# All eight gates of the mixer run inside its attention, in a written order of TensorE

## The chip, the cores and the metric

The kernel runs on one core of one Trainium2 chip. Its time is the device time of that core in microseconds (us); the median of three runs of the kernel before is 1740.22 us. The core has five instruction engines, each with an in-order queue: TensorE (PE in the profile; its weight loads are PEld), VectorE (DVE), ScalarE (ACT), GpSimd (POOL) and SyncE (SP).

## What is computed

One sequence of 256 tokens with 1024 features goes through two blocks, each with two layers. The first block has layers of retention, sliding-window attention and latent attention side by side, followed by a mixture of 16 experts. The second block has layers of a feed-forward network, a token mixer and another feed-forward network. The change is in the token mixer, and in two helpers that the first block uses too. Cut to the mixer, the reference is:

```python
def token_mixer(u, w_in, b_gate, attn_sink, pool_w, pool_scale, w_br_attn, w_br_pool, w_out, cos, sin):
    proj = u @ w_in
    q, k, v, p, ga, gb = jnp.split(proj, splits, axis=-1)   # 512, 128, 128, 512, 1024, 1024 columns
    q = partial_rope(q, cos, sin)
    k = partial_rope(k, cos, sin)
    y_attn = windowed_gqa(q, k, v, attn_sink) @ w_br_attn   # 8 heads, 2 key heads
    y_pool = multiscale_pool(p, pool_w, pool_scale) @ w_br_pool   # 4 groups of window means
    gate_a = jax.nn.sigmoid(ga + b_gate[:D_MODEL])
    gate_b = jax.nn.sigmoid(gb + b_gate[D_MODEL:])
    return (gate_a * y_attn + gate_b * y_pool) @ w_out
```

In the first block's retention the heads' outputs are normed and multiplied by `silu(g)` and a gain; and its queries and keys are rotated (`rope`) as the mixer's are.

## The kernel before

Weights. All weights lie in one flat fp32 array, in the order in which TensorE uses them; `recipe` (L50) writes that order down. SyncE loads them as tiles of up to 1 MB (`raw`). Each is cut into pieces of up to 1024 columns, and each piece is split into two reduced-precision halves: ScalarE's cast makes `whi` (L350), VectorE's subtraction makes `wlo` (L351). A product then is three matmuls, high by high, high by low, low by high (`mm3`, L413; the profile puts nearly all matmuls on L411, the line of `mm`, so they are told apart by their tiles). Five pieces are in flight; a cast waits until TensorE has used up an older piece.

The mixer (`mixer`, L1298), in the order of its text: normed and transposed input `xT_mx`; queries and keys (`oq`), rotated by `rope` (L625, first product on GpSimd, L628) into `q2r`; `q2r` is split into high and low halves `mT` for the scores, in two rounds j = 0, 1 of three casts on ScalarE (L1332, L1333, L1335) and two subtractions on VectorE (L1334, L1336); values and pooling input (`ovp`, then `vp`, L1341 and L1342). Then eight heads: scores `sc` (four matmuls), softmax (`softmax_head`, L586: masked scores and row extreme on VectorE, L597, exponential on ScalarE, L601, sum and division on VectorE, L608 to L613), four transposes of the probabilities `pt` (L1367), a copy to SBUF (`ptS`, L1371), and the head's output `po` (two matmuls). Two heads share an output bank, which is split into `aT`. Then the pooling, four groups: three matmuls into `opl`, a copy (`pl`, L1385), one matmul out, split into `pTm` (`split_evac`: L496 on ScalarE and L497 on VectorE). Then the gates and the branches: `gate(m)` (L1391) is 2 x 24 matmuls into `ogt`, a scaling on VectorE (L1396) and two tanh on ScalarE; `branch(m)` (L1404) is 12 matmuls over `aT` and 12 over `pTm` into `obr`, a gated product on VectorE (`mg`), the sum of its halves on GpSimd (`msum`, L1411), and a split into `mT`, which the output projection `wo2` (`oz`) reads. There are eight of both; `GATES_AHEAD = 4` sets four gates before the first branch.

The text is not the order on the engines. A scheduler of the framework orders the instructions of each engine by its own estimate of when their inputs are ready, with the order of the text as priority, so that the gates' matmuls, which depend on the input alone, fill the time in which TensorE would wait for softmaxes. Accumulator banks: 4 of the kind `acc` (`sc`, `pt`, `ovp`, `oz`), 2 `mm` (`ogt`, `obr`), 2 `tr` (`po`, `opl`).

The retention (in `attention1`, L633) makes the gate product from `th` (L812, VectorE) and the gain on GpSimd (`gg`, L813), then runs the scores `scr` and the decayed scores `sT` (L824, VectorE) into `oret`.

Of the kernel before, what the change touches and what calls it, by code (L numbers as in the profile page):

```python
# [30 lines left out]
NEG = -1e30  # L31
RAW = 2048
PIECE = 1024
GATES_AHEAD = 4
TAIL = 3
WARM = (24, 12, 60, 20)
LAG = 2
AFFINE_AT = (5, 7, 9, 11)
SCORES_AHEAD = 1
SWA_PERM = [0, 3, 1, 4, 2, 5]  # L40
GQA_PERM = [0, 4, 1, 5, 2, 6, 3, 7]
ROT_ORDER = [*range(8), *range(16, 40), *range(8, 16), *range(40, 64)]
OUT_ORDER = [5, 6, 7, 0, 1, 2, 3, 4]

# [5 lines left out]
def recipe():  # L50
    segs = []

    def wide(name, l, kts, n):
        for kt in kts:
            segs.append((name, l, kt * P, 0, n))

    def blocks(name, l, nkt, bs):
        for b in bs:
            for kt in range(nkt):
                segs.append((name, l, kt * P, b * P, P))  # L60

    for l in range(NL):
        if l == 0:
            for kt in range(0, 8, 2):
                wide("cq", l, range(kt, kt + 2), 384)
                segs.append(None)
        else:
            wide("cq", l, range(8), 384)
        wide("ckv", l, range(8), 288)
        blocks("rqk", l, 8, range(4))  # L70
        wide("vv", l, range(8), 384)
        blocks("uq", l, 3, range(5))
        blocks("ukn", l, 2, range(3))
        wide("ukv", l, range(2), 384)
        blocks("sqk", l, 8, range(4))
        wide("rg", l, range(8), 256)
        wide("wo", l, OUT_ORDER, D)
        segs.append(None)
        for e in range(NE):
            wide("gu", l * NE + e, range(8), 512)  # L80
            wide("dn", l * NE + e, range(2), D)
            segs.append(None)

    def ffn(i, l):
        for f in range(NF):
            blocks(f"f{i}w1", l, 8, [f])
            blocks(f"f{i}w3", l, 8, [f])
            wide(f"f{i}w2", l, [f], D)

    for l in range(NL):  # L90
        ffn(1, l)
        segs.append(None)
        blocks("qk2", l, 8, range(5))
        for kt in range(8):
            for n in range(2):
                segs.append(("vp2", l, kt * P, n * 320, 320))
        for m in range(8 + GATES_AHEAD):
            if m >= GATES_AHEAD:
                blocks("bra", l, 4, [m - GATES_AHEAD])
                blocks("brp", l, 4, [m - GATES_AHEAD])  # L100
            if m < 8:
                blocks("ga", l, 8, [m])
                blocks("gb", l, 8, [m])
        wide("wo2", l, range(8), D)
        segs.append(None)
        ffn(2, l)
        segs.append(None)
    return segs
# [258 lines left out]
def build(ctx: ExitStack, tc: tile.TileContext, ap, tap=None, parts=("b1", "b2")):  # L367
# [12 lines left out]
    def bank(tag, name):  # L380
        return ps.tile([P, 512], F32, name=name, tag=tag, bufs={"acc": 4, "mm": 2, "tr": 2}[tag])
# [14 lines left out]
    def col(name, l, j=None):  # L396
        o, w = COLS[name, l]
        return cols[:, o : o + w] if j is None else cols[:, o + j : o + j + 1]

    def rep(name, l):  # L400
        o, w = REPS[name, l]
        return reps[:, o : o + w]
# [7 lines left out]
    def mm(out, lhsT, rhs, start, stop):  # L410
        return TE.matmul(out, lhsT=lhsT, rhs=rhs, start=start, stop=stop)  # L411
# [213 lines left out]
    def rope(src, swapped, dst, cosT, sinT):  # L625

        shape = [P, src.shape[1], T]
        G.tensor_tensor(out=dst, in0=src, in1=cosT.unsqueeze(1).to_broadcast(shape), op=ALU.mult)  # L628
        V.tensor_tensor(out=swapped, in0=swapped, in1=sinT.unsqueeze(1).to_broadcast(shape), op=ALU.mult)
        return V.tensor_tensor(out=dst, in0=dst, in1=swapped, op=ALU.add)  # L630


    def attention1(l, x, hl, work, cb):  # L633
# [174 lines left out]
        for t in range(2):  # L808

            th = work.tile([P, 256], F32, name="th", tag="rp1", bufs=2)  # L810
            S.activation(out=th, in_=og[t][:, :256], func=AF.Tanh, scale=0.5)
            V.scalar_tensor_tensor(out=th, in0=th, scalar=1.0, in1=og[t][:, :256], op0=ALU.add, op1=ALU.mult)  # L812
            G.tensor_tensor(out=gg[:, t, :], in0=th, in1=rep("gn", l), op=ALU.mult)  # L813
        with tc.issue_after(W.split.ins), tc.issue_after(roped.ins):
            rope(rqk, swapped, rqk, cos64, sin64)
        oret = [bank("acc", f"oret{t}") for t in range(2)]
# [481 lines left out]
    def mixer(h, l, work, cb):  # L1298
# [46 lines left out]
        def scores(i):  # L1345
            b, j = divmod(i, 2)
            sc = bank("acc", "sc2")
            for t in range(2):
                o, c = sc[:, t * T : (t + 1) * T], slice(t * P, (t + 1) * P)
                mm(o, qs[j][:, b, c], ks[:, j], True, False)  # L1350
                mm(o, qs[j][half[j], b, c], kl[half[j]], False, True)
            return sc

        sc = [scores(i) for i in range(SCORES_AHEAD)]
        for b in range(4):
            out = bank("tr", "po2")
            for j in range(2):
                i = 2 * b + j
                if i + SCORES_AHEAD < 8:
                    sc.append(scores(i + SCORES_AHEAD))  # L1360
                pr = softmax_head(
                    work, sc[i], (T, T), (m0, m1), (nsc[:, 0:1], nsc[:, 1:2]), nsink[:, i : i + 1], rep("sink2", l)[:, i : i + 1], "g"
                )
                pt = bank("acc", "pt2")
                for jt in range(2):
                    for it in range(2):
                        TE.transpose(  # L1367
                            pt[:, jt * T + it * P : jt * T + (it + 1) * P], pr[:, it * T + jt * P : it * T + (jt + 1) * P], ident
                        )
                ptS = work.tile([P, 512], F32, name="ptS2", tag="w2k", bufs=2)  # L1370
                S.copy(ptS, pt)  # L1371
                o = out[j * 64 : (j + 1) * 64, :T]
                mm(o, vp[:, 0, half[j]], ptS[:, :T], True, False)
                mm(o, vp[:, 1, half[j]], ptS[:, T:], False, True)
            split_evac(aT[:, 0, b, :], aT[:, 1, b, :], out[:, :T])

        pT = work.tile([P, 2, 4, T], F32R, name="pTm", tag="pTm")
        for g in range(4):
            o = bank("tr", "opl")
            c = slice(P + g * P, P + (g + 1) * P)  # L1380
            mm(o[:, 0:136], vp[:, 0, c], pool[:, 0, g, :], True, False)
            mm(o[:, 120:136], vp[:, 1, c], pool[:, 1, g, :16], False, True)
            mm(o[:, 136:T], vp[:, 1, c], pool[:, 1, g, 16:], True, True)
            pl = work.tile([P, T], F32, name="pl", tag="w1k", bufs=2)
            S.copy(pl, o[:, :T])  # L1385
            mm(o[:, T:], pw[:, g, :], pl, True, True)
            split_evac(pT[:, 0, g, :], pT[:, 1, g, :], o[:, T:], col("pscale", l, g))

        gts = {}

        def gate(m):  # L1391
            o = bank("mm", "ogt")
            gemm_block("ga", hl, 8, o[:, :T])
            gemm_block("gb", hl, 8, o[:, T:])
            gt = work.tile([P, 512], F32, name="gt", tag="gt", bufs=GATES_AHEAD)
            V.tensor_tensor(  # L1396
                out=gt.rearrange("p (b t) -> p b t", b=2), in0=row.unsqueeze(1).to_broadcast([P, 2, T]),
                in1=o.rearrange("p (b t) -> p b t", b=2), op=ALU.mult,
            )
            S.activation(out=gt[:, :T], in_=gt[:, :T], func=AF.Tanh, scale=0.5, bias=hb[:, m : m + 1])  # L1400
            S.activation(out=gt[:, T:], in_=gt[:, T:], func=AF.Tanh, scale=0.5, bias=hb[:, 8 + m : 9 + m])
            gts[m] = gt

        def branch(m):  # L1404
            o = bank("mm", "obr")
            gemm_block("bra", (aT[:, 0], aT[:, 1]), 4, o[:, :T])
            gemm_block("brp", (pT[:, 0], pT[:, 1]), 4, o[:, T:])
            mg = work.tile([P, 512], F32, name="mg", tag="w2k", bufs=2)
            V.scalar_tensor_tensor(out=mg, in0=gts.pop(m), scalar=1.0, in1=o, op0=ALU.add, op1=ALU.mult)
            ms = work.tile([P, T], F32, name="msum", tag="w1k", bufs=2)  # L1410
            G.tensor_tensor(out=ms, in0=mg[:, :T], in1=mg[:, T:], op=ALU.add)  # L1411
            split_evac(ml[0][:, m, :], ml[1][:, m, :], ms, 0.5)

        for m in range(8 + GATES_AHEAD):
            if m >= GATES_AHEAD:
                branch(m - GATES_AHEAD)
            if m < 8:
                gate(m)
        oo = [[bank("acc", f"oz{t}{n}") for n in range(2)] for t in range(2)]
        gemm_wide(  # L1420
            "wo2", ml, 8, [[(oo[t][n], n * 512, (n + 1) * 512) for n in range(2)] for t in range(2)], tail=TAIL
# [110 lines left out]
```

## Time and profile before

| | |
|---|---|
| three runs | 1740.22 us median, 1735.24 to 1745.57 |
| profiled run | 1737.47 us, its span 1735.7 us |
| mean granted TensorE clock | 0.983 |
| TensorE busy | 1662.0 us, 96% |
| VectorE busy | 1251.6 us, 72% |
| ScalarE busy | 985.8 us, 57% |
| GpSimd busy | 62.4 us, 4% |
| DMA | 331.85 MB, mean 191 GB/s |

A time in the trace counts from the span's start. Of the 1735.7 us the two mixers' stretches from the first gate to the output projection begin at 873.6 (layer 0) and 1414.0 (layer 1). A row of the timeline gives the start, the length, the engine, the line, the instruction and the tiles out<-in; where several in a row are alike they are one row with a count, and the bracket behind it is the idle time before it and what ended that. The ends of matmuls are modelled, so a pace is better read from start to start. [...]

### The profile page before, as it was taken

What the parts mean: (1) busy time and instruction counts of PE and PEld (TensorE: products, weight loads), DVE (VectorE), ACT (ScalarE), POOL (GpSimd) and SP (SyncE); (2) the same over time, 40 slices, a digit from 0 to 9 for tenths busy, and PEclk for the clock granted to TensorE, in tenths of its full rate; (3) what the DMA queues carried; (4) which work ended last, traced back from release to release, by engine and by line L of the source; (5) the groups of instructions that cost most, each with busy time, mean ns of one, the idle gap of its engine ahead of it and who ended that gap; (6) DMA issues with size and microseconds to landing.
All of it is one profiled execution on the core that took longest, in us unless ns stands there. A gap on an engine that the chain in (4) does not pass through costs nothing.

```text
span 1735.7 us, 24721 instructions
## 1 busy us (share of the span) xinstructions
PE 1662.0 (96%) x9258; PEld 1407.9 (81%) x9258; DVE 1251.6 (72%) x2268; ACT 985.8 (57%) x1643; POOL 62.4 (4%) x54
## 2 busy tenths in 40 slices
PE   8998999899999979999999999998999999999997
PEld 7877777797777758888889888887888798978886
DVE  5768999876789997666675666667666766666665
ACT  5646777564577755555475555555555565555553
POOL 0001000200100010000000100000000000100000
PEclk9998999999899989999999999999999999999999
DMA  9432999543278965555433545554555442545540
GB/s 379 148 120 100 339 335 347 189 169 122 74 296 335 333 224 199 179 189 189 153 129 132 189 164 185 191 194 146 190 182 186 166 161 90 188 176 194 191 149 25
DMA packets 49421, 331.85 MB, mean 191 GB/s; under 512 B 5648, under 2 KB 5904, under 8 KB 13712
## 3 DMA queue, kind: packets, MB, share of 16 engines
q1 hardware_dynamic: 47952, 325.73, 52.2%
q10 hardware_dynamic: 1344, 4.49, 0.9%
q8 instruction: 75, 1.23, 0.3%
q14 instruction: 50, 0.41, 0.1%
HBM read 326.79 MB, written 1.05 MB: 189 GB/s over the span
## 4 chain that ended last, share of the span: by engine, by line
PE 66%; DVE 3%; ACT 2%; issue 1%; ACTq 0%; DVEq 0%
PE v L411 14%; PE u L411 14%; PE f L411 14%; PE ogt L411 6%; PE ogu L411 4%; PE obr L411 3%; PE oz L411 2%; PE yg L411 2%; PE ovp L411 2%; PE oq L411 2%; PE sc L411 1%; PE po L411 1%; DVE wlo L351 1%; ACT junk L537 1%; PE opl L411 1%
## 5 line engine op out<-in xcount | busy, mean ns | idle before, releaser
L351 DVE TENSOR_TENSOR wlo<-raw,whi 128x1024 fp32r<-128x1024 f32 (+2 forms) x611 | 736.6, 1212 | 351.7 <-ACT whi L350 345.8
L350 ACT CAST whi<-raw 128x1024 fp32r<-128x1024 f32 (+2 forms) x611 | 629.7, 1034 | 533.5 <-PE v L411 125.8
L411 PE MATMUL f<-whi,fhh 128*128 128x512 f32 x704 | 233.0, 392 | 4.3 <-ACT fhh L1284 4.3
L411 PE MATMUL u<-xT_f,whi 128*128 128x512 f32 x528 | 191.1, 401 | 4.0 <-DVE xT_f L497 4.0
L411 PE MATMUL v<-xT_f,whi 128*128 128x512 f32 x528 | 189.9, 399 | 0.0
L411 PEld LDWEIGHTS f<-whi,fhh 128*128 128x128 f32 x704 | 132.1, 188 | 36.6 <-ACT fhh L1284 6.0
L411 PE MATMUL u<-xT_f,wlo 128*128 128x256 f32 x528 | 149.0, 282 | 0.0
L411 PE MATMUL v<-xT_f,wlo 128*128 128x256 f32 x528 | 148.3, 281 | 0.0
L411 PE MATMUL f<-wlo,fhh 128*128 128x512 f32 x352 | 138.1, 392 | 0.0
L411 PEld LDWEIGHTS u<-xT_f,whi 128*128 128x128 f32 x528 | 100.1, 190 | 28.2 <-DVE xT_f L497 4.7
L411 PEld LDWEIGHTS v<-xT_f,whi 128*128 128x128 f32 x528 | 99.2, 188 | 24.7
L411 PE MATMUL ogu<-wlo,xgh 128*128 128x512 f32 x256 | 102.2, 399 | 3.9 <-DVE wlo L351 3.9
L411 PE MATMUL ogu<-whi,xgh 128*128 128x512 f32 x256 | 102.8, 402 | 0.1
L411 PEld LDWEIGHTS u<-xT_f,wlo 128*128 128x128 f32 x528 | 100.5, 190 | 2.4
L411 PE MATMUL ogu<-whi,xgl 128*128 128x512 f32 x256 | 101.2, 395 | 0.0
L411 PEld LDWEIGHTS v<-xT_f,wlo 128*128 128x128 f32 x528 | 99.8, 189 | 0.0
L411 PE MATMUL ogt<-xT_mx,whi 128*128 128x256 f32 x512 | 97.4, 287 | 0.0
L411 PE MATMUL yg<-whi,hh 128*128 128x512 f32 x256 | 84.9, 393 | 2.9 <-ACT hh L493 2.8
L411 PEld LDWEIGHTS ogt<-xT_mx,whi 128*128 128x128 f32 x512 | 80.4, 191 | 3.0 <-issue 1.5
L411 PEld LDWEIGHTS f<-wlo,fhh 128*128 128x128 f32 x352 | 66.1, 188 | 10.5
L411 PE MATMUL ogt<-xT_mx,wlo 128*128 128x256 f32 x256 | 73.0, 286 | 0.0
L411 PE MATMUL u<-x2hl,whi 128*128 128x512 f32 x176 | 64.7, 406 | 6.2 <-DVE x2hl L584 6.2
(555 smaller groups left out, 3078.9 us busy)
## 6 DMA issues: line engine op xcount, KB each, us to landing
raw<-in_wflat_dram SPq DMA_DIRECT2D x276, 1024.0 KB, 4.8
raw<-in_wflat_dram SPq DMA_DIRECT2D x10, 960.0 KB, 4.6
gb<-in_rows_dram SPq DMA_DIRECT2D x8, 512.0 KB, 4.7
raw<-in_wflat_dram SPq DMA_DIRECT2D x4, 992.0 KB, 4.8
raw<-in_wflat_dram SPq DMA_DIRECT2D x4, 512.0 KB, 3.4
raw<-in_wflat_dram SPq DMA_DIRECT2D x2, 1008.0 KB, 6.3
raw<-in_wflat_dram SPq DMA_DIRECT2D x2, 976.0 KB, 6.9
raw<-in_wflat_dram SPq DMA_DIRECT2D x4, 384.0 KB, 5.9
```

Of the source, the lines that this page charges most:

```text
L350: nc.scalar.copy(hi[:, :n], r[:, c : c + n])
L351: self.split = nc.vector.tensor_tensor(out=lo[:, :n], in0=r[:, c : c + n], in1=hi[:, :n].bitcast(F32), op=ALU.subtract)
L411: return TE.matmul(out, lhsT=lhsT, rhs=rhs, start=start, stop=stop)
L537: S.activation(out=junk(), in_=h[:, t, n * 512 : (n + 1) * 512], func=AF.Square, accum_out=ss[:, n : n + 1])
```

## The change

The order of TensorE from the first gate to the last branch is now written out by hand, under `tc.manual_schedule(engines={mybir.EngineType.PE})`; the other engines' order is still the scheduler's. The gates are cut in halves `ga` and `gb` and set around the parts of a head: for head i, the scores of head i+1, on every second head the pooling into its bank, `gb` of gate i, pooling out, the transposes of head i, `ga` of gate i+1, the output of head i. After head 7's transposes come two pool branches, the last output, and then the branches in the order of `BRANCHES`. The flat weight array follows in that order, and a branch's bank takes the pool half first. The first product of the rotation, the retention's `gg` and the branch sum `msum` move from GpSimd to VectorE. Gates have eight buffers instead of four. A smaller scratch area for dynamic DMAs, which this kernel has none of from GpSimd, frees memory.

```diff
-GATES_AHEAD = 4
...
-SCORES_AHEAD = 1
...
+BRANCHES = [("brp", 0), ("brp", 1), ("bra", 0), ("bra", 1)] + [(k, m) for m in range(2, 8) for k in ("brp", "bra")]
@@ -94,13 +93,11 @@
         for kt in range(8):
             for n in range(2):
                 segs.append(("vp2", l, kt * P, n * 320, 320))
-        for m in range(8 + GATES_AHEAD):
-            if m >= GATES_AHEAD:
-                blocks("bra", l, 4, [m - GATES_AHEAD])
-                blocks("brp", l, 4, [m - GATES_AHEAD])
-            if m < 8:
-                blocks("ga", l, 8, [m])
-                blocks("gb", l, 8, [m])
+        for m in range(8):
+            blocks("ga", l, 8, [m])
+            blocks("gb", l, 8, [m])
+        for k, m in BRANCHES:
+            blocks(k, l, 4, [m])
         wide("wo2", l, range(8), D)
         segs.append(None)
         ffn(2, l)
@@ -625,7 +622,7 @@
     def rope(src, swapped, dst, cosT, sinT):
 
         shape = [P, src.shape[1], T]
-        G.tensor_tensor(out=dst, in0=src, in1=cosT.unsqueeze(1).to_broadcast(shape), op=ALU.mult)
+        V.tensor_tensor(out=dst, in0=src, in1=cosT.unsqueeze(1).to_broadcast(shape), op=ALU.mult)
         V.tensor_tensor(out=swapped, in0=swapped, in1=sinT.unsqueeze(1).to_broadcast(shape), op=ALU.mult)
         return V.tensor_tensor(out=dst, in0=dst, in1=swapped, op=ALU.add)
 
@@ -810,7 +807,7 @@
             th = work.tile([P, 256], F32, name="th", tag="rp1", bufs=2)
             S.activation(out=th, in_=og[t][:, :256], func=AF.Tanh, scale=0.5)
             V.scalar_tensor_tensor(out=th, in0=th, scalar=1.0, in1=og[t][:, :256], op0=ALU.add, op1=ALU.mult)
-            G.tensor_tensor(out=gg[:, t, :], in0=th, in1=rep("gn", l), op=ALU.mult)
+            V.tensor_tensor(out=gg[:, t, :], in0=th, in1=rep("gn", l), op=ALU.mult)
         with tc.issue_after(W.split.ins), tc.issue_after(roped.ins):
             rope(rqk, swapped, rqk, cos64, sin64)
         oret = [bank("acc", f"oret{t}") for t in range(2)]
@@ -1351,16 +1348,67 @@
                 mm(o, qs[j][half[j], b, c], kl[half[j]], False, True)
             return sc
 
-        sc = [scores(i) for i in range(SCORES_AHEAD)]
-        for b in range(4):
-            out = bank("tr", "po2")
-            for j in range(2):
-                i = 2 * b + j
-                if i + SCORES_AHEAD < 8:
-                    sc.append(scores(i + SCORES_AHEAD))
+        pT = work.tile([P, 2, 4, T], F32R, name="pTm", tag="pTm")
+        gts = {}
+
+        def pool_in(g):
+
+            o = bank("tr", "opl")
+            c = slice(P + g * P, P + (g + 1) * P)
+            mm(o[:, 0:136], vp[:, 0, c], pool[:, 0, g, :], True, False)
+            mm(o[:, 120:136], vp[:, 1, c], pool[:, 1, g, :16], False, True)
+            mm(o[:, 136:T], vp[:, 1, c], pool[:, 1, g, 16:], True, True)
+            pl = work.tile([P, T], F32, name="pl", tag="w1k", bufs=2)
+            S.copy(pl, o[:, :T])
+            return o, pl
+
+        def pool_out(g, o, pl):
+            mm(o[:, T:], pw[:, g, :], pl, True, True)
+            split_evac(pT[:, 0, g, :], pT[:, 1, g, :], o[:, T:], col("pscale", l, g))
+
+        def gate(m, o):
+            gt = work.tile([P, 512], F32, name="gt", tag="gt", bufs=8)
+            V.tensor_tensor(
+                out=gt.rearrange("p (b t) -> p b t", b=2), in0=row.unsqueeze(1).to_broadcast([P, 2, T]),
+                in1=o.rearrange("p (b t) -> p b t", b=2), op=ALU.mult,
+            )
+            S.activation(out=gt[:, :T], in_=gt[:, :T], func=AF.Tanh, scale=0.5, bias=hb[:, m : m + 1])
+            S.activation(out=gt[:, T:], in_=gt[:, T:], func=AF.Tanh, scale=0.5, bias=hb[:, 8 + m : 9 + m])
+            gts[m] = gt
+
+        obr = {}
+
+        def branch(k, m):
+            if k == "brp":
+                obr[m] = bank("mm", "obr")
+                gemm_block("brp", (pT[:, 0], pT[:, 1]), 4, obr[m][:, T:])
+                return
+            o = obr.pop(m)
+            gemm_block("bra", (aT[:, 0], aT[:, 1]), 4, o[:, :T])
+            mg = work.tile([P, 512], F32, name="mg", tag="w2k", bufs=2)
+            V.scalar_tensor_tensor(out=mg, in0=gts.pop(m), scalar=1.0, in1=o, op0=ALU.add, op1=ALU.mult)
+            ms = work.tile([P, T], F32, name="msum", tag="w1k", bufs=2)
+            V.tensor_tensor(out=ms, in0=mg[:, :T], in1=mg[:, T:], op=ALU.add)
+            split_evac(ml[0][:, m, :], ml[1][:, m, :], ms, 0.5)
+
+
+        with tc.manual_schedule(engines={mybir.EngineType.PE}):
+            og = bank("mm", "ogt")
+            gemm_block("ga", hl, 8, og[:, :T])
+            ahead = scores(0)
+            for i in range(8):
+                b, j = divmod(i, 2)
+                sc, ahead = ahead, scores(i + 1) if i < 7 else None
                 pr = softmax_head(
-                    work, sc[i], (T, T), (m0, m1), (nsc[:, 0:1], nsc[:, 1:2]), nsink[:, i : i + 1], rep("sink2", l)[:, i : i + 1], "g"
+                    work, sc, (T, T), (m0, m1), (nsc[:, 0:1], nsc[:, 1:2]), nsink[:, i : i + 1], rep("sink2", l)[:, i : i + 1], "g"
                 )
+                if j == 0:
+                    pooled = pool_in(b)
+                gemm_block("gb", hl, 8, og[:, T:])
+                gate(i, og)
+                if j == 0:
+                    pool_out(b, *pooled)
+                    out = bank("tr", "po2")
                 pt = bank("acc", "pt2")
                 for jt in range(2):
                     for it in range(2):
@@ -1369,53 +1417,19 @@
                         )
                 ptS = work.tile([P, 512], F32, name="ptS2", tag="w2k", bufs=2)
                 S.copy(ptS, pt)
+                if i < 7:
+                    og = bank("mm", "ogt")
+                    gemm_block("ga", hl, 8, og[:, :T])
+                else:
+                    branch(*BRANCHES[0])
+                    branch(*BRANCHES[1])
                 o = out[j * 64 : (j + 1) * 64, :T]
                 mm(o, vp[:, 0, half[j]], ptS[:, :T], True, False)
                 mm(o, vp[:, 1, half[j]], ptS[:, T:], False, True)
-            split_evac(aT[:, 0, b, :], aT[:, 1, b, :], out[:, :T])
-
...
-        for m in range(8 + GATES_AHEAD):
-            if m >= GATES_AHEAD:
-                branch(m - GATES_AHEAD)
-            if m < 8:
-                gate(m)
+                if j == 1:
+                    split_evac(aT[:, 0, b, :], aT[:, 1, b, :], out[:, :T])
+            for k, m in BRANCHES[2:]:
+                branch(k, m)
         oo = [[bank("acc", f"oz{t}{n}") for n in range(2)] for t in range(2)]
         gemm_wide(
             "wo2", ml, 8, [[(oo[t][n], n * 512, (n + 1) * 512) for n in range(2)] for t in range(2)], tail=TAIL
@@ -1519,7 +1533,7 @@
     import concourse.bacc as bacc
     from concourse.bass_utils import run_bass_kernel_spmd
 
-    nc = bacc.Bacc("TRN2", target_bir_lowering=False, num_devices=1)
+    nc = bacc.Bacc("TRN2", target_bir_lowering=False, num_devices=1, dynamic_dma_scratch_size=1024)
     arrays, ap = {}, {}
     for name, v in host_arrays(inputs).items():
         arrays[f"in_{name}_dram"] = v
```

TensorE before, in the mixer of layer 0 from the middle of gate 0 to the first head's output (`sc_9090`, `sc_9096`, `sc_9124` are the scores of heads 0, 1 and 2, `pt` the transposed probabilities, `po` a head's output, `ogt` the gate):

```order
L411 MATMUL sc_9090<-mT 128x256 x4
L411 MATMUL ogt<-xT_mx,whi 128x256
...
L411 MATMUL sc_9096<-mT 128x256 x4
...
L1367 MATMUL pt_9115<-cperm,pr_g 128x128
L411 MATMUL sc_9124<-mT 128x256
L1367 MATMUL pt_9115<-cperm,pr_g 128x128 x3
L411 MATMUL sc_9124<-mT 128x256 x3
...
L411 MATMUL po_9095<-ptS_9120,vp 64x256 x2
L1367 MATMUL pt_9143<-cperm,pr_g 128x128 x4
```

TensorE now, same place, from the end of the first half of gate 0 (`sc_9122`, `sc_9127`, `sc_9228` are the scores of heads 0, 1 and 2, `opl` the pooling, whose constants `cb_6990` holds):

```order
L408 MATMUL ogt<-xT_mx,wlo 128x256
L408 MATMUL sc_9122<-mT 128x256 x4
L408 MATMUL sc_9127<-mT 128x256 x4
L408 MATMUL opl<-cb_6990,vp 128x136
L408 MATMUL opl<-cb_6990,vp 128x16
L408 MATMUL opl<-cb_6990,vp 128x120
L408 MATMUL ogt<-xT_mx,whi 128x256 x2
...
L408 MATMUL opl<-pl,pw 128x256
L1415 MATMUL pt_9190<-cperm,pr_g 128x128 x4
...
L408 MATMUL po_9189<-ptS_9195,vp 64x256 x2
L408 MATMUL sc_9228<-mT 128x256 x4
```

The scores of heads 0 and 1 now stand back to back behind 24 gate matmuls, with the first pooling behind them; the transposes of head 0 stand right behind the pooling's last product, and the scores of head 2 behind the first head's output.

VectorE before, in the same place, from the last of head 1's row extremes on (`gt` is the scaled gate, `den_g`, `rec_g` and `pr_g` the softmax's sum, its reciprocal and the probabilities):

```order
L597 ISA pr_g,nm_g<-sc_9096,cb_6990,nsink_8768,nsc 128x256
L597 ISA nm_g 128x1
L1396 TENSOR_TENSOR gt<-row,ogt 128x512
L351 TENSOR_TENSOR wlo<-raw,whi 128x1024
L608 TENSOR_TENSOR den_g<-den_g,es_g 128x2
L351 TENSOR_TENSOR wlo<-raw,whi 128x1024
L609 RECIPROCAL rec_g<-den_g 128x2
L608 TENSOR_TENSOR den_g<-den_g,es_g 128x2
L351 TENSOR_TENSOR wlo<-raw,whi 128x1024
L613 TENSOR_SCALAR pr_g<-pr_g,rec_g 128x256 x2
```

VectorE now, same place (`pTm` is the low half of the pooled group's split):

```order
L594 ISA pr_g,nm_g<-sc_9127,cb_6990,nsink_8768,nsc 128x256
L594 ISA nm_g 128x1
L348 TENSOR_TENSOR wlo<-raw,whi 128x1024
L605 TENSOR_TENSOR den_g<-den_g,es_g 128x2
L1371 TENSOR_TENSOR gt<-row,ogt 128x512
L606 RECIPROCAL rec_g<-den_g 128x2
L494 SCALAR_TENSOR_TENSOR pTm<-opl,cols,pTm 128x256
L610 TENSOR_SCALAR pr_g<-pr_g,rec_g 128x256 x2
```

The gate's scaling moved from ahead of the softmax's sum to between the sum and its reciprocal, and the pooled group's split came in ahead of the division of head 0's probabilities; two of three weight splits went from this place.

## Rows read from the trace of the kernel before

**Rows 1.** Busy times by window: us, each engine, granted clock, DMA share, GB/s.

```profile
873.60:970.20 96.60, 96.60 (x706) 86.28 (x705) 62.47 (x126) 58.40 (x116) 4.76 (x7) 1.00 0.36 126
1414.00:1510.70 96.70, 96.70 (x707) 86.38 (x706) 62.18 (x124) 57.57 (x115) 4.81 (x7) 1.00 0.36 124
960.00:970.00 10.00, 10.00 (x86) 10.00 (x85) 6.36 (x9) 5.31 (x8) 1.60 (x3) 1.00 0.51 176
```

**Rows 2.** Timeline of TensorE: a gate's first matmuls, then two branches' first (start, us).

```profile
953.09 0.40 PE L411 MATMUL ogt<-xT_mx,whi 128*128 128x256 f32 x2
...
958.84 0.40 PE L411 MATMUL obr<-aT,whi 128*128 128x256 f32 x2
...
961.69 0.40 PE L411 MATMUL obr<-aT,whi 128*128 128x256 f32 x2
```

**Rows 3.** Timeline of TensorE: a head's small products, and a pooling group's.

```profile
889.16 1.08 PE L411 MATMUL po<-ptS,vp 128*64 128x256 f32 x4
...
890.17 0.66 PE L1367 MATMUL pt<-cperm,pr_g 128*128 128x128 f32 x4
890.58 1.30 PE L411 MATMUL sc<-mT 128*128 128x256 f32 x4
...
915.18 0.94 PE L411 MATMUL opl<-cb,vp 128*128 128x136 f32 x6
...
915.88 0.36 PE L411 MATMUL ogt<-xT_mx,wlo 128*128 128x256 f32 x1
...
916.80 0.60 PE L411 MATMUL opl<-pl,pw 128*128 128x256 f32 x2
```

**Rows 4.** Timeline of TensorE: layer 0's first gate matmuls and first scores.

```profile
873.62 0.40 PE L411 MATMUL ogt<-xT_mx,whi 128*128 128x256 f32 x2
...
877.70 1.22 PE L411 MATMUL sc<-mT 128*128 128x256 f32 x4
```

**Rows 5.** Timeline of ScalarE: the weight cast ahead of the query's copies.

```profile
873.38 1.05 ACT L350 CAST whi<-raw 128x1024 fp32r<-128x1024 f32 x1 [2.03 <-PE ovp L411]
```

**Rows 6.** Timeline of VectorE: the query's splits, head 0's softmax, gate 0's scaling.

```profile
876.26 1.22 DVE L1336 TENSOR_TENSOR mT<-q2r,mT 64x1024 fp32r<-64x1024 f32 x1 [0.61 <-ACT mT L1335]
...
878.16 1.22 DVE L1336 TENSOR_TENSOR mT<-q2r,mT 64x1024 fp32r<-64x1024 f32 x1 [0.24 <-ACT mT L1335]
...
879.88 0.54 DVE L597 CUSTOM_DVE_ANT_0 pr_g<-sc,cb,nsink 128x256 f32<-128x256 f32 x1
...
882.09 0.68 DVE L1396 TENSOR_TENSOR gt<-row,ogt 128x512 f32<-128x512 f32 x1
...
886.30 0.61 DVE L613 TENSOR_SCALAR pr_g<-pr_g,rec_g 128x256 f32<-128x256 f32 x2
```

**Rows 7.** The pooling's tile by instruction: count, ns min/median/max, first and last start.

```profile
L496 ACT ACTIVATE pTm<-opl,cols x8: 467/474/475, 917.5 to 1467.1; 128x256 fp32r<-128x256 f32 x8
L497 DVE SCALAR_TENSOR_TENSOR pTm<-opl,cols,pTm x8: 477/484/484, 918.0 to 1468.4; 128x256 fp32r<-128x256 f32 x8
```

**Rows 8.** Timeline: retention of the first block's layer 1, before the head outputs.

```profile
405.56 0.75 DVE L812 SCALAR_TENSOR_TENSOR th<-th,og 128x256 f32<-128x256 f32 x2
...
406.22 0.55 DVE L824 TENSOR_TENSOR sT<-scr,cb 128x384 f32<-128x384 f32 x1
...
406.83 0.88 PE L411 MATMUL oret<-vv,sT 128*128 128x64 f32 x6 [0.48 <-DVE sT L824]
```

**Rows 9.** Timeline of GpSimd and VectorE: the mixer's rotation and weight splits beside it.

```profile
860.38 2.97 POOL L628 TENSOR_TENSOR q2r<-q,cb 128x1280 f32<-128x1280 f32 x1 [214.02 <-DVE q L1320]
...
860.65 4.79 DVE L351 TENSOR_TENSOR wlo<-raw,whi 128x960 fp32r<-128x960 f32 x2 [0.48 <-ACT whi L350]
...
865.36 1.48 DVE L629 TENSOR_TENSOR q2s<-q2s,cb 128x1280 f32<-128x1280 f32 x1
...
866.76 1.21 DVE L351 TENSOR_TENSOR wlo<-raw,whi 128x1024 fp32r<-128x1024 f32 x1
```

**Rows 10.** Busy times by window, at the entry of the mixer in layers 0 and 1.

```profile
844.00:846.00 2.00, 2.00 (x12) 2.00 (x11) 1.44 (x8) 1.39 (x4) 0.00 (x0) 0.50 0.00 0
1384.00:1386.00 2.00, 1.45 (x11) 1.28 (x12) 2.00 (x14) 0.95 (x3) 0.00 (x0) 1.00 0.00 0
```

More of the change, by code (lines that the diff above doesn't have):

```diff
@@ L1374, in mixer @@
                 mm(o, vp[:, 1, half[j]], ptS[:, T:], False, True)
-            split_evac(aT[:, 0, b, :], aT[:, 1, b, :], out[:, :T])
[L1377 to L1412, printed above, removed]
```

## The prediction

> **What bounds the kernel now.** I read first the busy time by engine: TensorE 96% of the span, VectorE 72%, ScalarE 57%, GpSimd 4%. So TensorE sets the time, and an edit counts only if it gives TensorE less work, takes away one of its waits, or adds one. Then I read the two stretches that the change rewrites, the mixer of layer 0 and of layer 1 from the first gate to the output projection: 96.6 us each, TensorE busy in all of it at a granted clock of 1.00, VectorE busy 62 us and the DMA engines 0.36 of the time [rows 1]. The reader is to see that nothing is waited for there: no wait can be taken out of these stretches, only new ones put in.
>
> The third look is at what "busy" hides, since an end of a matmul is modelled. Start to start, a gate of 48 matmuls takes 958.84 - 953.09 = 5.75 us (0.12 us each), a branch 961.69 - 958.84 = 2.85 us [rows 2]. Eight of both are 68.8 us. The small products: a head's output 1.01 us, the transposes 0.41, the scores 1.22, so 2.64 a head and 21.1 for eight; the pooling 0.70 into the bank and at most 0.60 out of it, 5.2 for four groups [rows 3, 4]. Together 95.1; the other 1.5 us of 96.6 are what some 19 interruptions of the gate stream cost, about 0.08 us each.
>
> **TensorE's work after.** The same matmuls, none more or less. In the new order the stream of gate and branch blocks is interrupted 16 times a layer: -3 x 0.08 = -0.2 us, -0.4 for both layers. Bounds: all 1.5 us of both layers gone, -3; or as much again, +3. I take -0.4, by the 0.08 just found.
>
> **The start of the attention, where the order is now fixed.** Before, the scheduler put each head's products where their inputs were ready, with gate matmuls between. Now TensorE has to take: the first half of gate 0, scores 0, scores 1, the first pooling, the second half of gate 0, pooling out, transposes 0. Times of layer 0:
>
> 1. Scores 0. The half gate begins at 873.62 [rows 4] and ends 24 x 0.12 = 2.87 later, at 876.5. The scores need the second part of q's split, which ended at 876.26 + 1.22 = 877.48 and was itself released by ScalarE [rows 6]. ScalarE was late since a weight cast stands ahead of q's copies in its queue and waited 2.03 us for the value projection to free a piece [rows 5]; neither the cast nor its place changes. The scheduler put the scores at 877.70 [rows 4] and filled up with gate matmuls; the written order can't. Wait: 877.55 - 876.5 = 1.05 us.
> 2. Scores 1 follow 1.22 later, at 878.75, but use the other half of q: 878.16 + 1.22 = 879.4 [rows 6]. Wait: 0.7.
> 3. Transposes 0. Scores 1 end at 880.65, the pooling at 881.35, the half gate at 884.2, pooling out at 884.8. The probabilities could be ready by then (row maxima 0.54 us each from scores 0 at 878.8, and before the first head had 6.4 us from its first maximum at 879.88 to its division at 886.30, other work between [rows 6]). But VectorE's new queue has two instructions ahead of the division: gate 0's scaling (0.68 us, from 884.2) and the second half of the pooled group's split, which waits for pooling out at 884.8, then 0.47 us on ScalarE and 0.48 on VectorE [rows 6, 7]: 885.75. The division of both halves takes 0.61: 886.35. Wait: 886.35 - 884.8 = 1.55. Behind the waiting transpose stand gate 1 and all the rest; no other engine is short of work by it.
>
> Sum 3.3 us a layer. Layer 1 runs the same program on the same row lengths, so 6.6 for two. Bounds from the same rows: nothing at all (the splits and the division just in time, as every head's were before [rows 1]), or twice, 13, if each wait also takes the 2.03 of the cast's wait with it. I take 6.6; with the -0.4 it is 6.2.
>
> **The heads that follow** cost nothing, and this is what hides them: between a head's scores and its transposes TensorE now has half a gate, transposes, half a gate, a head's output, scores and half a gate: 2.87 + 0.41 + 2.87 + 1.01 + 1.22 + 2.87 = 11.3 us. The softmax before took 6.4 with weight splits between its steps [rows 6]. Without that cover each head would cost its lateness (rival C).
>
> **The branches at the end.** Without gates between them, eight branches make VectorE's densest stretch. The last four stood alone before as well: in 960 to 970 VectorE was busy 6.36 of 10 us [rows 1]. The branch sum is new on it: 10/2.85 = 3.5 an interval, at the 0.48 of the nearest row of that shape [rows 7] 1.7 us, so 8.1 of 10: still free. The sum leaves GpSimd, which did three in that interval in 1.60 us; nobody on TensorE waited for them. The weight pieces are not short: the cast waits for TensorE to free a piece, not for data [rows 5], and the DMA engines are at 0.51 of their time [rows 1]; the stream's new order moves no byte more. Cost 0. Bounds 0 to +3 us, one branch's time, should the first attention branch come before its last head is split. The four more gate buffers and the smaller scratch hold no work of an engine: 0.
>
> **The two moves of the retention.** The swish product, now on VectorE, stands between the row maths on `th` and the first decay product `sT`. TensorE waits there already: 0.48 us for `sT` at 406.83, behind two `th` instructions that took 406.22 - 405.56 = 0.66 in all [rows 8]. Two products of the same shape at that price add 0.66 to that wait in layer 1. In layer 0 the wait was smaller and I take half: 0.33. Together 1.0 (bounds 0, if gate weights split elsewhere give the room, to 1.5).
>
> **The rotation.** GpSimd took 2.97 us for the mixer's first product; meanwhile two weight splits of 960 columns took 4.79 us on VectorE where one of 1024 takes 1.21 [rows 9]. So the engine that was to be relieved lost 4.79 - 2.3 = 2.5 us. The same product on VectorE is 1.48 by the sister row [rows 9], so VectorE gains about 1 us. [...] It is worth nothing in the sum, since the wait that follows is set by ScalarE's cast [rows 5], not by VectorE; two of these in the mixers and two in the first block. Bounds -2 (1 us each where it counts, on one layer of each block) to +1.
>
> **Sum** against the profiled run: 1737.5 + 6.2 + 1.0 = 1744.7. The median shown, 1740.2, lies 2.7 above that run, so I predict 1747.
>
> **Rivals.**
>
> A. The waits don't come, or are paid back: VectorE, rid of the contention, reaches the splits sooner and TensorE enters the heads as smoothly as before. For it: the 2.5 us above, and that every head was hidden before [rows 1]. Against it: the splits wait on ScalarE, and the order of the queues. Then the sum is -0.4 to +1.0 with up to -2 for the rotation: 1739, between 1734 and 1742. It is also the case in which the change doesn't do what it says: TensorE has no idle time there for gates to fill.
>
> B. The new gaps bring the clock down. At the mixer's entry of layer 0 TensorE has gaps of this size, and the granted clock was 0.50 in 844 to 846 after them; in layer 1 the same gaps kept 1.00 [rows 10]. [...]
>
> C. Slower, by late softmaxes: the written order stops TensorE at every head if VectorE's queue puts a division behind a gate's scaling and weight splits. The place is the transposes of heads 1 to 7, 14 in two layers; the price 0.5 us, nearly one scaling [rows 6], each: +7, 1754. It decides from the point where a softmax takes 11.3 us; before it took 6.4, hence improbable.
>
> **How the numbers follow.** Forecast 55% (1742 to 1752), A 22%, B 15% (1748 to 1756), C 8% (1750 to 1760). The range 1736 to 1757 leaves out the lower part of A and the upper parts of B and C. What a measurement of this kernel tells from no change is about 0.5%, so 1731.5 and 1748.9. Faster than that would need all bounds of gain at once: 7%. Slower: a third of the forecast, most of B and C: 36%. The rest, 57%, within.
>
> **What would show it.** In the profile after: TensorE idle before `sc` released by VectorE's q split, about 1 and 0.7 us; before the first `pt`, released by the division, about 1.5 us, at the start of both attentions and nowhere later; `oret` waiting about 1.1 us in layer 1; no GpSimd row in the mixers; weight splits at 1.2 us beside the rotation. From the first gate to the output projection 99.7 instead of 96.6 us. I am wrong if these stretches are no longer than before, if waits come at later heads or in the branches, or if the clock falls in them.

## The result and the profile after

| | before | after |
|---|---|---|
| median | 1740.30 us (8 runs, 1735.01 to 1745.57) | 1753.36 us (8 runs, 1749.80 to 1757.63) |
| profiled run | 1737.47 us, clock 0.983 | 1757.63 us, clock 0.975 |

The changed kernel is slower: ratio 1.0073, 95% interval 1.0057 to 1.0089, or 12.7 us. The profiled run lost more, 20.2 us, and a part of that is luck: it was the slowest of its eight runs, and the profiled run before was below the median. So the trace says where time was lost, and only repeated runs say how much.

The page of the changed kernel shows as much TensorE time as before in share, more in microseconds, and GpSimd halved (busy us, share, instructions):

```profile
PE 1677.3 (96%) x9258; PEld 1419.2 (81%) x9258; DVE 1261.0 (72%) x2292; ACT 985.4 (56%) x1643; POOL 34.6 (2%) x30
```

The same 9258 matmuls are 15 us longer, and the mean granted clock is 0.975 instead of 0.983: where busy time rises and the count doesn't, look at the clock by stretches. The two mixers from the first gate to `wo2`, then three stretches inside them and in the retention (window, busy times, granted clock as a share of full speed, DMA share, GB/s; compare [rows 1]):

```profile
880.08:981.68 101.60, 98.71 (x706) 87.96 (x705) 66.34 (x133) 58.21 (x116) 0.00 (x0) 0.98 0.36 120
1427.74:1530.75 103.01, 100.11 (x707) 88.98 (x705) 66.00 (x131) 58.34 (x116) 0.00 (x0) 0.97 0.34 116
886.00:892.00 6.00, 6.00 (x31) 5.49 (x32) 4.63 (x12) 4.31 (x12) 0.00 (x0) 0.72 0.41 124
1432.00:1442.00 10.00, 9.32 (x40) 7.67 (x39) 6.34 (x15) 6.06 (x15) 0.00 (x0) 0.66 0.31 107
412.00:422.00 10.00, 9.36 (x35) 7.48 (x32) 2.92 (x9) 0.00 (x0) 0.00 (x0) 0.55 0.32 105
```

The mixers took 101.6 and 103.0 us instead of 96.6. TensorE is idle for 2.9 of it in each (101.60 - 98.71), and it ran part of the rest at a lower clock: 6 us at 0.72 are 1.7 us lost, 10 us at 0.66 are 3.4. 96.6 + 2.9 + 1.7 = 101.2, and 96.6 + 2.9 + 3.4 = 102.9; 0.1 to 0.4 remains, which these windows don't explain. The waits themselves, in layer 0:

```profile
883.99 1.32 PE L408 MATMUL sc<-mT 128*128 128x256 f32 x4 [0.87 <-DVE mT L1333]
885.99 1.29 PE L408 MATMUL sc<-mT 128*128 128x256 f32 x4 [0.68 <-DVE mT L1333]
887.22 1.41 PE L408 MATMUL opl<-cb,vp 128*128 128x136 f32 x6
...
892.41 0.59 PE L408 MATMUL opl<-pl,pw 128*128 128x256 f32 x2
894.35 0.81 PE L1415 MATMUL pt<-cperm,pr_g 128*128 128x128 f32 x4 [1.35 <-DVE pr_g L610]
```

They are where the forecast put them: 0.87, 0.68 and 1.35 us for a predicted 1.05, 0.7 and 1.55. The slow stretch begins at the end of the second wait or just behind it, and is over before the third. Behind the third, the longest, the clock stays at 1.00, in layer 0 as in layer 1 (where the third ends at 1443.4):

```profile
887.00:891.00 4.00, 4.00 (x20) 3.87 (x21) 3.63 (x9) 3.33 (x11) 0.00 (x0) 0.57 0.38 88
892.00:900.00 8.00, 6.65 (x43) 5.07 (x42) 5.92 (x12) 3.92 (x7) 0.00 (x0) 1.00 0.48 169
1433.00:1441.00 8.00, 7.35 (x30) 6.48 (x31) 5.26 (x13) 5.08 (x13) 0.00 (x0) 0.57 0.39 134
1441.00:1450.00 9.00, 7.65 (x50) 5.94 (x49) 6.53 (x15) 3.94 (x8) 0.00 (x0) 1.00 0.43 131
```

VectorE's queue at the third shows its cause, the gate's scaling and the pooled split ahead of the division:

```profile
892.61 0.69 DVE L1371 TENSOR_TENSOR gt<-row,ogt 128x512 f32<-128x512 f32 x1 [1.98 <-PE ogt L408]
...
893.55 0.48 DVE L494 SCALAR_TENSOR_TENSOR pTm<-opl,cols,pTm 128x256 fp32r<-128x256 f32 x1 [0.18 <-ACT pTm L493]
...
893.95 0.61 DVE L610 TENSOR_SCALAR pr_g<-pr_g,rec_g 128x256 f32<-128x256 f32 x2
```

Over the whole span TensorE's waits for these releasers are (us in total, times, longest):

```profile
PE sc L408 <- DVE mT L1333: 3.1, 4, 0.9
PE oret L408 <- DVE sT L821: 2.9, 4, 1.2
PE pt L1415 <- DVE pr_g L610: 2.7, 2, 1.3
```

The first and the third did not exist before; the second was

```profile
PE oret L411 <- DVE sT L824: 1.3, 3, 0.6
```

No later head and no branch waits. In the retention of layer 1 the gain product stands between `th` and `sT` as forecast, and lengthens the wait of [rows 8] from 0.48 to 1.15 us:

```profile
409.35 0.75 DVE L810 TENSOR_TENSOR gg<-th,reps 128x256 f32<-128x256 f32 x2
410.02 0.55 DVE L821 TENSOR_TENSOR sT<-scr,cb 128x384 f32<-128x384 f32 x1
...
410.62 0.88 PE L408 MATMUL oret<-vv,sT 128*128 128x64 f32 x6 [1.15 <-DVE sT L821]
```

Behind it comes the slow stretch 412 to 422, which no step of the forecast had: from `scr` to `trr` the retention of layer 1 took 432.35 - 407.79 = 24.6 us, before 423.88 - 404.66 = 19.2. Layer 0's retention has a slow stretch too, and took 20.8 us from `scr` to `trr` instead of 18.3:

```profile
99.00:102.00 3.00, 3.00 (x12) 2.61 (x11) 0.98 (x2) 0.00 (x0) 0.00 (x0) 0.51 0.04 11
```

The rotation, last, went as its rows let expect; beside it the two weight splits of 960 columns took 1.15 and 1.16 us instead of 4.79 together [rows 9]. Nothing came of that: from the first `oq` to the first gate TensorE took 1414.08 - 1382.27 = 31.8 us in layer 1 before, and 880.08 - 848.26 = 31.8 in layer 0 now, both at a clock of 1.00.

```profile
866.73 1.49 DVE L625 TENSOR_TENSOR q2r<-q,cb 128x1280 f32<-128x1280 f32 x1
...
868.14 1.15 DVE L348 TENSOR_TENSOR wlo<-raw,whi 128x960 fp32r<-128x960 f32 x1
...
870.53 1.16 DVE L348 TENSOR_TENSOR wlo<-raw,whi 128x960 fp32r<-128x960 f32 x1 [1.24 <-ACT whi L347]
```

### The profile page after: what moved, and what is told of

The parts are those of the page before. It is cut to its first block, busy times and chain, and to the rows that moved or that the text cites. A ratio compares the mean times of both kernels' runs of the same rounds, so it can differ in the third digit from the quotient of the medians.

```text
span 1755.8 us, 24673 instructions
## 1 busy us (share of the span) xinstructions
PE 1677.3 (96%) x9258; PEld 1419.2 (81%) x9258; DVE 1261.0 (72%) x2292; ACT 985.4 (56%) x1643; POOL 34.6 (2%) x30
## 3 DMA queue, kind: packets, MB, share of 16 engines
HBM read 326.79 MB, written 1.05 MB: 187 GB/s over the span
## 4 chain that ended last, share of the span: by engine, by line
PE 66%; DVE 3%; ACT 2%; issue 1%; ACTq 0%; DVEq 0%
PE u L408 14%; PE v L408 14%; PE f L408 14%; PE ogt L408 5%; PE ogu L408 4%; PE obr L408 3%; PE oz L408 2%; PE yg L408 2%; PE oq L408 2%; PE ovp L408 2%; PE sc L408 1%; PE po L408 1%; DVE wlo L348 1%; PE opl L408 1%; ACT whi L347 1%
## 5 line engine op out<-in xcount | busy, mean ns | idle before, releaser
L408 PEld LDWEIGHTS v<-xT_f,whi 128*128 128x128 f32 x528 | 99.2, 188 | 24.6
L408 PE MATMUL ogu<-whi,xgl 128*128 128x512 f32 x256 | 101.6, 397 | 0.0
```

## The experiments

Theory 1: the loss is the new waits and slow stretches that they bring on. Theory 2: the waits alone; slow stretches fall by luck, as often without them. Theory 3: a steady cost of the written order or of VectorE's new work.

**The moves alone.** `G.` becomes `V.` for rotation, gain product and branch sum; the order stays the scheduler's.

```diff
-        G.tensor_tensor(out=dst, in0=src, in1=cosT...
+        V.tensor_tensor(out=dst, in0=src, in1=cosT...
-            G.tensor_tensor(out=gg[:, t, :], in0=th...
+            V.tensor_tensor(out=gg[:, t, :], in0=th...
-            G.tensor_tensor(out=ms, in0=mg[:, :T]...
+            V.tensor_tensor(out=ms, in0=mg[:, :T]...
```

> Only the three moves from GpSimd to VectorE, on the kernel before. Theory 1 (the loss is the new waits and the slow clock that they bring on): both retentions wait some 0.6 us more for sT and their clock falls to 0.50 for some microseconds afterwards; mixers stay at 96.6 us; +2 to +7 us in all, ratio 1.001 to 1.004. Theory 2 (the waits alone; the clock falls as often without them): +1.3 us, ratio 1.001, no slow stretch in the retentions that the kernel before doesn't have. Theory 3 (a steady cost of VectorE's added work): the mixers are longer too, each 1 us or more.

1743.28 us, ratio 1.0018 (1.0000 to 1.0037). The mixers are as before, layer 1's retention is slow, and layer 0's stays at 1.00:

```profile
879.51:976.06 96.55, 96.55 (x707) 86.28 (x705) 65.23 (x133) 58.23 (x116) 0.00 (x0) 1.00 0.37 126
1420.08:1516.61 96.53, 96.53 (x706) 86.27 (x705) 64.87 (x131) 57.46 (x116) 0.00 (x0) 1.00 0.36 123
410.00:422.00 12.00, 11.36 (x40) 9.03 (x40) 3.61 (x11) 0.00 (x0) 0.00 (x0) 0.50 0.24 87
```

VectorE does the branch sums and the rotation, and the mixers are not a tenth longer: theory 3 falls for them, and the 5 to 6 us of each mixer belong to the written order.

**The gain product back on GpSimd**, all else as changed.

> The changed kernel with the retention's gain product back on GpSimd. Theory 1: 3 to 8 us less than the changed kernel, ratio to the kernel before 1.003 to 1.006, the retentions at a clock of 1.00 as before. Theory 2: 1.3 us less, ratio 1.0065. Theory 3: no less, 1.007.

1750.77 us, ratio 1.0054 (1.0032 to 1.0076). Over all runs its mean is 4.0 us (2.4 to 5.7) below the changed kernel's; the waits that it takes away are 2.9 - 1.3 = 1.6 us. Its mixers have the waits, and both are slow; its retention isn't, in either layer (layer 1 shown last):

```profile
871.00:972.60 101.60, 98.70 (x707) 87.96 (x706) 66.35 (x133) 58.24 (x116) 0.00 (x0) 0.98 0.35 120
1417.60:1519.19 101.59, 98.69 (x707) 87.85 (x705) 66.00 (x131) 58.24 (x116) 0.00 (x0) 0.98 0.35 117
400.00:424.00 24.00, 22.16 (x133) 17.66 (x132) 16.50 (x52) 9.00 (x18) 2.73 (x3) 1.00 0.30 104
```

**Half a gate more ahead.** Both halves of gate 0 stand ahead of the first scores, and each later half one place earlier; the first pool branch takes the place that comes free at head 7.

```diff
+            half_gate()
+            half_gate()
             ahead = scores(0)
...
-                gemm_block("gb", hl, 8, og[:, T:])
-                gate(i, og)
+                half_gate()
...
-                if i < 7:
-                    og = bank("mm", "ogt")
-                    gemm_block("ga", hl, 8, og[:, :T])
-                else:
-                    branch(*BRANCHES[0])
-                    branch(*BRANCHES[1])
+                half_gate()
```

> The changed kernel with the second half of gate 0 ahead of the first scores, and every later half gate one place earlier. Theory 1: no wait for the first two scores, a wait of at most 0.7 us before the first transposes, no slow clock: mixers 96.6 to 97.5 us instead of 101.6 and 103.0, 8 to 11 us less than the changed kernel, ratio to the kernel before 1.001 to 1.003. Theory 2: 5 us less, ratio 1.0045, slow stretches as before. Theory 3: mixers stay above 99 us at a clock of 1.00.

1748.03 us, ratio 1.0033 (1.0014 to 1.0052); in the mean 7.0 us (4.7 to 9.3) below the changed kernel. That is less than the 8 to 11 expected and than the 10.3 that the two mixers differ by in the profiles (101.60 - 97.15 and 103.01 - 97.14). Both waits for scores are gone, 0.52 us is left at the first transposes, and the clock holds:

```profile
879.82:976.97 97.15, 96.63 (x706) 86.30 (x705) 66.13 (x133) 58.58 (x116) 0.00 (x0) 1.00 0.37 125
1425.33:1522.47 97.14, 96.62 (x706) 86.30 (x705) 65.78 (x131) 58.57 (x116) 0.00 (x0) 1.00 0.37 123
```

96.63 us busy is the time of before: the order costs TensorE's own work nothing, and gains none either.

**Idle matmuls in the waits.** TensorE waits as long, but multiplies zeros meanwhile, ahead of scores 0, scores 1 and transposes 0.

```diff
+            fillers(7)
             ahead = scores(0)
...
+                if i == 0:
+                    fillers(5)
                 sc, ahead = ahead, scores(i + 1) if i < 7 else None
...
                 pt = bank("acc", "pt2")
+                if i == 0:
+                    fillers(10, pt)
```

> The changed kernel with idle matmuls on zeros in its three waits of each mixer (7, 5 and 10 of 256 columns): TensorE waits as long but is busy meanwhile. Theory 1: the clock stays at 1.00 there, mixers about 99.6 us (96.6 and the 2.9 of waits) instead of 101.6 and 103.0, 3 to 5 us less than the changed kernel in all, ratio 1.0045 to 1.0055. Theory 2: the same slow stretches and the same time as the changed kernel, 1.007. Theory 3: as theory 2.

1751.20 us, ratio 1.0055 (1.0034 to 1.0077). The windows of its two mixers:

```profile
875.74:975.80 100.06, 99.68 (x729) 88.40 (x728) 66.33 (x133) 58.21 (x116) 0.00 (x0) 1.00 0.36 122
1419.80:1519.84 100.04, 99.66 (x728) 88.39 (x727) 65.97 (x131) 58.22 (x116) 0.00 (x0) 1.00 0.35 119
```

3.45 us above before, at a clock of 1.00. Of it 3.29 lie between the first idle matmul of each wait and the product behind it (1.02, 0.76 and 1.51), here in layer 0:

```profile
878.62 0.94 PE L408 MATMUL idle<-zeros 128*128 128x256 bf16 x7
879.64 1.32 PE L408 MATMUL sc<-mT 128*128 128x256 f32 x4
880.89 0.72 PE L408 MATMUL idle<-zeros 128*128 128x256 bf16 x5
881.65 1.29 PE L408 MATMUL sc<-mT 128*128 128x256 f32 x4
...
886.96 1.25 PE L408 MATMUL pt<-zeros 128*128 128x256 bf16 x10
888.47 0.81 PE L1426 MATMUL pt<-cperm,pr_g 128*128 128x128 f32 x4 [0.26 <-DVE pr_g L610]
```

To size the clock's part in the mean the pair was run again on one chip:

> The kernel with idle matmuls in the mixers' waits once more, beside the changed kernel on the same chip, to size the clock's share in the mean over many runs. Theory 1: both mixers at 1.00 and 100.05 us again, 2 to 4 us less than the changed kernel in the mean. Theory 2: no difference in the mean; a slow stretch in a mixer may show.

> The changed kernel a third time, for comparison in the mean and a third profile. Theory 1: slow stretches in both mixers again. Theory 2: at least one of the two mixers without.

1753.36 us, 1.0070 (1.0045 to 1.0095), and 1754.89 us, 1.0084 (1.0063 to 1.0104). The changed kernel's mixers were slow once more (clock 0.98 and 0.97), the filled ones 100.1 us at 1.00. Over all runs, 18 against 16, filling gains 2.5 us (0.3 to 4.6). The mixers of the profiles differ by 4.5 (101.60 - 100.06 and 103.01 - 100.04), the upper end of that interval; whether the slow stretches stand in every run without a profile too is not shown.

**Both kernels again**, unchanged, for second profiles:

> The changed kernel once more, for a second profile. Theory 1 (the waits bring on the slow clock at their place): both mixers and the second layer's retention show a granted clock of 0.50 for some microseconds again, mixers 101.5 to 103 us, retention 5 us longer than before. Theory 2 (slow stretches fall anywhere, by luck): at least two of these three places at 1.00 this time.

> The kernel before once more, for a second profile. Both theories: mixers 96.6 us at a clock of 1.00. Theory 1: the retentions at 1.00 too. Theory 2: some slow stretch in a mixer or a retention is as likely as in the changed kernel.

1755.70 us, ratio 1.0075 (1.0051 to 1.0100), and 1742.87 us in one run. The changed kernel's mixers took 101.57 and 103.08 us with the same slow stretches. The kernel before had clean mixers, but a slow retention in layer 1:

```profile
876.24:972.85 96.61, 96.61 (x707) 86.28 (x706) 62.47 (x126) 58.43 (x116) 4.80 (x7) 1.00 0.36 126
1417.50:1514.10 96.60, 96.60 (x707) 86.29 (x705) 62.19 (x124) 57.50 (x115) 4.80 (x7) 1.00 0.36 124
412.00:420.00 8.00, 8.00 (x27) 6.56 (x28) 4.50 (x18) 0.00 (x0) 0.00 (x0) 0.57 0.16 67
```

So theory 1 has to be told apart by place. In the mixers it holds: 8 of 8 profiled with the three idle waits are slow, at a mean clock of 0.97 or 0.98 (the changed kernel three times, and once with `gg` on GpSimd), 0 of 16 without them, all at 1.00 (filled, with half a gate ahead, or in the scheduler's order, the repaired kernels below included). In all 8 the stretch begins between the end of the second wait and 1.8 us behind it, and ends before the third wait, so it goes with the first two, and not with the longest; which of the two, or both together, no run tells apart. In layer 0's retention a slow stretch stood in 4 of 7 profiles with the longer wait and in 0 of 5 without it. In layer 1's it stood in all 7, and also in 2 of 5 without: there a slow stretch is likelier with the longer wait, and comes without it too.

**Both repairs.** Half a gate ahead, with the gain product on GpSimd, or on VectorE but behind the first `sT`:

```diff
-            V.tensor_tensor(out=gg[:, t, :], in0=th, in1=rep("gn", l), op=ALU.mult)
+            ths.append(th)
...
+        for t in range(2):
+            V.tensor_tensor(out=gg[:, t, :], in0=ths[t], in1=rep("gn", l), op=ALU.mult)
         ro = work.tile([P, 2, 256], F32, name="ro", tag="ckv")
```

> Both repairs: half a gate more ahead of the first scores, and the retention's gain product back on GpSimd; rotation and branch sum stay on VectorE. Theory 1: all waits but 1 us are gone, mixers 97.15, retentions as before: +1 us, ratio to the kernel before 0.999 to 1.002. Theory 2: the same +1 us from the waits. Theory 3 (a steady cost of the order or of VectorE's added work): 1.003 or more.

> Half a gate more ahead of the first scores, and the gain product on VectorE, but behind the first decay product instead of ahead of it. Theory 1: as with the product on GpSimd, retentions at 1.00 and not longer than before, ratio 0.999 to 1.002: it was the place in VectorE's order, not the engine. Rival: the product on VectorE costs wherever it stands, ratio 1.003 as in the kernel with half a gate ahead alone.

1743.04 us, 1.0005 (0.9991 to 1.0019), and 1742.81 us, 1.0004 (0.9990 to 1.0019). Both are the time of the kernel before within what can be measured, so the two places account for the whole loss, to within some 3 us (the upper ends of the intervals). By the second the engine did not matter, only the place in its queue: the wait is 0.48 us again, as in [rows 8].

```profile
405.15 0.74 DVE L810 SCALAR_TENSOR_TENSOR th<-th,og 128x256 f32<-128x256 f32 x2
405.81 0.55 DVE L822 TENSOR_TENSOR sT<-scr,cb 128x384 f32<-128x384 f32 x1
406.28 0.75 DVE L829 TENSOR_TENSOR gg<-th,reps 128x256 f32<-128x256 f32 x2
406.41 0.88 PE L408 MATMUL oret<-vv,sT 128*128 128x64 f32 x6 [0.48 <-DVE sT L822]
```

That the retentions would stay at 1.00, as expected, failed: a window of the same profile shows a slow stretch behind the short wait in layer 1, the second of the two counted above:

```profile
410.00:418.00 8.00, 8.00 (x25) 6.23 (x25) 2.67 (x9) 0.00 (x0) 0.00 (x0) 0.50 0.28 117
```

No run points to a version that beats the kernel before: with all but 0.52 us of the new waits gone, a mixer is still 96.6 us of TensorE's work.

## Why the prediction was right, and where it was short

The direction and the range held (1753.36 in 1736 to 1757); the forecast of 7 us was about half of the 12.7. The main case, 1742 to 1752, was missed, and the likeliest outcome (57%) was no change that can be told. The range held because it made room for rivals B and C.

- *TensorE's work does not shrink.* Right: 96.62 us busy with half a gate ahead, 96.6 before. The 0.2 us a layer for fewer interruptions did not show.
- *Three waits a layer, 3.3 us.* Right: 2.9 us idle, and mixers 3.45 us longer at full clock (filled kernel): 6.9 us for both layers, where the forecast had 6.6.
- *Heads and branches covered.* Right: no wait at any later head or branch. Rival C did not occur.
- *Retention, 1.0 us.* The mechanism was right and the size in layer 1 exact (0.67 for 0.66). Layer 0 was taken at half, 0.33, and paid 0.95 from `scr` to `trr` (the moves alone, clock 1.00), most of it in a wait of 0.64 for a second `sT` that was not there before: 1.6 us in all, as the waits for `sT` say, just above the upper bound of 1.5.
- *Rotation and branch sum: nothing.* Right, by the moves alone: mixers 96.55 and 96.53, and 31.8 us from the first `oq` to the first gate. Rival A's gain, weight splits of 2.31 us in all beside the rotation instead of 4.79, did not reach TensorE.
- *The clock.* This is the step that fell short. The sum put it at nothing and left it to rival B, with a chance of 15%, between 1748 and 1756. That range rests on a price of 2 us for a slow stretch in each mixer, which no run shows; the stretches of the profile after lost 1.7 us in layer 0's mixer and 3.4 in layer 1's (6 us at 0.72, 10 us at 0.66). B is what happened in the mixers: the clock fell to 0.97 or 0.98 in every profiled mixer with the three waits, which the prediction itself had named as a sign of being wrong. Its price in the mean is 2.5 us (0.3 to 4.6) in the mixers, by filling the waits. In the retention, where neither forecast nor rival looked for it, the product's move costs 4.0 us (2.4 to 5.7) by one pair of kernels and 5.3 (3.1 to 7.5) by the other (half a gate ahead against both repairs). 1.6 of that is the wait; the rest, 2.4 to 3.7 by difference, goes with the slow stretches.

The sum as it should have been: 6.9 + 1.6 in waits, 2.5 + 2.4 to 3.7 in clock, 13.4 to 14.7; measured 12.7, by the interval 9.9 to 15.5. Pooled over all chips, 18 runs of the changed kernel have a mean of 1754.5 us and a mean clock of 0.9771, and 63 of the kernel before 1741.5 and 0.9796. The difference of 13.0 leaves 4.5 us beside the waits, and 4.6 us more of the clock were withheld (1754.5 x 0.0229 - 1741.5 x 0.0204, an estimate; not all of it need fall where TensorE sets the time). So the clock's part is 4 to 6 us. The repairs say it in another way: 7.0 us come back with half a gate ahead and some 5 with the gain product. The moves alone cost only 3 us by the ratio (0 to 6), though layer 1's retention in their profile lost 6.6; one profile is one throw.

What stays open is how much of the retention's 2.4 to 3.7 us the longer wait brings on, since the same stretch is slow in some runs of the kernel before; and why one place is slow in every profile and another in some. Open too is why waits of 0.87 and 0.68 us were followed by a slow stretch in 8 of 8 mixers, and the wait of 1.35 us behind them in none: the length of a wait alone did not decide. The forecast had a sign of it in hand, the 0.50 of [rows 10] behind gaps like those it was adding, and set the 1.00 of layer 1 against it.

Zeros multiplied in the waits kept the clock at 1.00 in 4 of 4 mixers. The mean clock of one program varied from run to run: the kernel before alone spread from 1735.0 us at a mean clock of 0.986 to 1746.7 at 0.975.

## What to carry to other kernels

Where an engine is busy without a gap, as TensorE was here for 96.60 of 96.60 us, an order written by hand has little to win (96.63 us busy with half a gate ahead): before writing it, list for each step when its inputs were ready under the scheduler, and keep enough independent work ahead of the first step whose inputs come late. Here the new waits, 8.5 us of TensorE (6.9 in the mixers, 1.6 in the retentions), came with 4 to 6 more in clock; if a wait can't be avoided, idle matmuls in it are worth a try (in the mixers they held 1.00 and gave back 2.5 us; in the retention it was not tried). And an instruction moved to another engine can land between two that the bottleneck waits for, as `gg` did here (a wait of 1.15 us instead of 0.48); look at its neighbours in the new queue, not at the engine's load.

## What the runs showed of the hardware

In a mixer's three waits 22 bf16 matmuls of 256 columns on zeros kept a clock of 1.00 in 4 of 4 mixers, where the same waits idle gave 0.97 and 0.98 in 8 of 8. The length of a wait alone did not tell whether a slow stretch followed: behind 0.87 and 0.68 us it came in 8 of 8 mixers, behind 1.35 us in none. The slow stretches of one program came and went at one place (layer 0's retention in 2 of 3 profiles of the changed kernel, 0.51 in the first, 1.00 in the third) and stood in every profile at another (its mixers, 6 of 6). And the kernel before differed by 0.7% between runs as its mean clock did (1735.0 us at 0.986, 1746.7 at 0.975), as much as this change.
